# A first phase cut into other segments, sums in contiguous columns, and unread products on TensorE

## The chip, the cores and the metric

The kernel runs on one core of a Trainium2 chip. The metric is the time of one execution on the device, in microseconds (us). Three runs of the kernel before gave 1920.49, 1921.16 and 1923.17, so the median is 1921.16.

## What is computed

One layer of a hybrid decoder, for 256 prompt tokens and 8 samples of 8 tokens, 320 tokens in all (NT). The model width is 2048: 16 tiles (T) of 128 channels.

```python
mod = silu(c) @ ada_w + ada_b               # six sections of 2048: shift, scale, gate, twice
h   = rmsnorm(x, norm_mix_w) * (1 + sc_m) + sh_m
p   = h @ w_in                              # GLU value | GLU gate | z | x,B,C (3072 columns) | dt
xbc, new_sconv = causal_dwconv(xbc, st_sconv, ssm_conv_w, ssm_conv_b)   # 4 taps
y   = gated_rmsnorm(ssd_scan(silu(xbc), dt, ...), z)
v   = silu(layernorm(causal_dwconv(glu(value, gate))))                   # 31 taps
x   = x + g_m * (concat[v, y] @ w_out)
x   = x + g_f * conv_ffn(rmsnorm(x) * (1 + sc_f) + sh_f)
return rmsnorm(x), ...                      # and the last rows of each convolution, the SSD states
```

The outputs that carry the convolution states (`new_sconv` among them) hold the last three raw rows of x/B/C.

## The kernel before

**Products.** All data is fp32. Each weight tile is split into a high part (`whi`, ScalarE casts at L298 and L299, one for each half of its columns) and a low part (`wlo`, VectorE subtractions at L303 and L304), each h tile into `HQh` and `HQl`. A tile of 128 by 128 weights takes three matmuls of 320 columns: high by high (L378), high by low (L379), low by high (L380).

**The stream.** All weight loads stand in one list, `stream`. SyncE issues them in this order as soon as a buffer of the `raw` pool is free, and TensorE takes its work in the same order. There are two kinds of entry. A *unit* (kind "w") is a weight load of up to 2048 columns with its split and its matmuls. A *piece* (kind "ada") is a load of ada_w columns and unsplit matmuls of it with silu(c) into the bank `adaq` (L439).

**The first phase.** The scale and shift of an h tile must be known before h can be formed, so the kernel works by segments of h tiles, listed in `SEGS` as (first tile, number): 1, 3, 4, 4 and 4 tiles. For each segment there are pieces for its shift and scale (`KPIECE` k-slices in each, so 16/KPIECE pieces), then a chain that forms its h tiles, then units that multiply these tiles with their rows of the x/B/C weights. There are 24 output tiles; a unit holds `NUNIT` of them as *groups*, each group a sum over the segment's tiles in one of four `acc` banks of PSUM. The string of a segment in `orders` gives the stream: W is one of this segment's units, A one of the next segment's pieces. In the segments of 3 and 4 tiles the last A is followed by two W.

**The chain.** When the last piece is done, `chain` goes ahead of the other background work: a transpose and three small operations on VectorE (L446 to L452), then `modulated` (L230 to L244), which multiplies x by scale and by rstd, adds shift, lets ScalarE write `HQh` and VectorE write `HQl`. `bg.drain` places the steps of the background between the split of the next unit and the evictions: a unit first evicts what the unit before left, splits the next unit's weights, drains, and then issues its matmuls. `finish` in `pre` of the next segment's first unit makes sure that its h is formed.

**Evictions.** `xbc_evac` adds a group's bank into `extZ` (output tiles 0 to 13) or `extV` (14 to 23, named `rv` in the trace). There a tile has 347 columns: 3 of left padding, 256 of the prompt, and 8 samples with 3 state columns and 8 tokens each. So an eviction is two instructions, one of 256 columns (L516, L519) and one of 64 (L517, L520), copies on ScalarE in the first segment, additions on VectorE in the others. Groups but the last four of a unit are evicted two groups later (`each`), the last four at the start of the next unit. `pads` fills the state columns with two large GpSimd copies at the start of the last segment. In the last segment each second eviction adds the 4-tap convolution of two output tiles to the background (`xbc_conv`). The dt projection (`dt_product`, L580) runs ahead of the last segment's first unit.

Of the kernel before, what the change touches and what calls it, by code (L numbers as in the profile page):

```python
# [41 lines left out]
V0, C0 = VOFF["nfw"][0], COFF["idn"][0]  # L42


SEGS = [(0, 1), (1, 3), (4, 4), (8, 4), (12, 4)]

KPIECE = {1: 8, 3: 2, 4: 2}
NUNIT = {1: 6, 3: 4, 4: 4}
LAST = len(SEGS) - 1

POOLED = (2, 6)

# [53 lines left out]
def kernel(ctx: ExitStack, tc: tile.TileContext, A: dict):  # L106
# [48 lines left out]
    class Stats:  # L155
# [20 lines left out]
        def rstd(self, eps, collect=True):  # L176
# [3 lines left out]
            V.reciprocal(r, r)  # L180
            return r

    class Sums:


# [101 lines left out]
            slots.append(e["slot"])  # L287
        pump()

    def split(e, bgq=0.0):  # L290
        if "hi" in e:
            return
        w = e["w"]
        e["hi"] = sb.tile([128, w], F32R, tag="whi", name="whi", bufs=2)
        e["lo"] = sb.tile([128, w], F32R, tag="wlo", name="wlo", bufs=2)
        hw = (w // 256) * 128
        r0, r1 = e["raw"](0, hw), e["raw"](hw, w - hw)
        S.copy(e["hi"][:, :hw], r0)  # L298
        S.copy(e["hi"][:, hw:], r1)  # L299
        E = e.get("lo_on", V)  # L300
        if bgq and E is V:
            bg.drain(bgq)
        E.tensor_tensor(e["lo"][:, :hw], r0, e["hi"][:, :hw].bitcast(F32), op=ALU.subtract)  # L303
        E.tensor_tensor(e["lo"][:, hw:], r1, e["hi"][:, hw:].bitcast(F32), op=ALU.subtract)  # L304
        if bgq and E is G:
            bg.drain(bgq)
        release_raw(e)
# [22 lines left out]
    def run_stream():  # L330
# [7 lines left out]
        for n, e in enumerate(stream):  # L338
# [21 lines left out]
                bg.drain(0.65 * b)  # L360
            else:
                bg.drain(b)
            if "hi" not in e:
                split(e)
            xo = e["x"]() if callable(e["x"]) else e["x"]
            hi, lo = e["hi"], e["lo"]
            banks = []
# [18 lines left out]
                    pend.append(lambda f=e["each"], i=i, b=banks[i]: f(i, b))  # L386
            if e.get("evac"):
                pend.append(lambda f=e["evac"], bk=banks: f(bk))
            if m is not None and "hi" not in stream[m] and "raw" in stream[m]:
                split(stream[m])  # L390
            if e.get("post"):
                e["post"]()
# [31 lines left out]
    def ada_segment_entries(si):  # L424
# [18 lines left out]
        def chain():  # L443
            ps = get()
            md = scr("md")
            V.transpose(md[:, :w], ps[:, :w])  # L446
            m4 = md[:, :w].rearrange("p (s t r) -> p s t r", s=2, t=n)
            sc, sh = mods["s1"][:, t0:t0 + n, :], mods["sh1"][:, t0:t0 + n, :]
            bc = [128, n, 9]
            V.tensor_tensor(sc, m4[:, 0, :, 0:9], cv("adb", 16 + t0, n).unsqueeze(2).to_broadcast(bc), op=ALU.add)  # L450
            V.tensor_tensor(sh, m4[:, 1, :, 0:9], cv("adb", t0, n).unsqueeze(2).to_broadcast(bc), op=ALU.add)
            V.scalar_tensor_tensor(sc, sc, 1.0, cv("nmw", t0, n).unsqueeze(2).to_broadcast(bc),  # L452
                                   op0=ALU.add, op1=ALU.mult)
            yield 1.0
            if t0 % 4 == 0:
                box["parts"] = new_quarter(t0 // 4)
            box.setdefault("h", [None] * T)
            yield from modulated(t0, n, box["rstd_x"], mods["s1"], mods["sh1"], box["htmp"], box["h"], box["parts"])

        def post():  # L460
            bg.items.insert(0, [f"hq{si}", chain(), 0])
            if si == 0:
                bg.finish("hq0")

        np_ = T // kp
        for pc in range(np_):
# [42 lines left out]
    def xbc_evac(tb, q):  # L509
        def go(i, bank):  # L510
            tt = tb + i
            ext = xt_ext(tt)
            p, s, st = ext_views(ext, 3, 11)
            bs = v3(bank[:, NPR:NT], LS)
            if q == 0:
                S.copy(p, bank[:, :NPR])  # L516
                S.copy(s, bs)  # L517
            else:
                V.tensor_tensor(p, p, bank[:, :NPR], op=ALU.add)  # L519
                V.tensor_tensor(s, s, bs, op=ALU.add)  # L520
            if q == LAST and i % 2 == 1:
                bg.add("xconv" if tt >= 14 else "xconvz", xbc_conv(tt - 1))
                if tt == 13:
                    SP.dma_start(A["osc"][:, 0:14, :], box["extZ"][:, :, 256:347])
                if tt == 23:
                    SP.dma_start(A["osc"][:, 14:24, :], box["extV"][:, :, 256:347])
# [583 lines left out]
    with tc.manual_schedule():  # L1110
# [29 lines left out]

        aq = [ada_segment_entries(i) for i in range(len(SEGS))]

        st = Stats()
        for q, tag in enumerate(("HQh2", "HQl2", "HQh3", "HQl3")):
            sq = sb.tile([128, 4, NT], F32, tag=tag, name="sq" + tag)
# [17 lines left out]
        stream.extend(aq0)  # L1163
        hget = lambda: box["h"]
        NX = 24
        orders = ["WAAWAAWAAAWA", "WAAAAWWAAWAAWW", "AWAAWAAWAAWAWW", "AWAAWAAWAAWAWW", "WWWWWW"]
        W1 = A["w1"]
        for si, (t0, n) in enumerate(SEGS):
            nxt = list(aq[si + 1]) if si + 1 < len(SEGS) else []
# [2 lines left out]
            for ch in orders[si]:  # L1172
# [7 lines left out]
                def pre(si=si, g=g, t0=t0, n=n):  # L1180
                    if g == 0:
                        bg.finish(f"hq{si}")
                        if t0 + n in (8, 12):
                            raw_retire(f"q{(t0 + n) // 4}")
                    if (si, g) == (LAST, 0):
                        raw_retire("bc")
                    if (si, g) == (LAST, 1):
                        raw_retire("xs")
                    if (si, g) == (LAST, 0):
                        pads()  # L1190
# [11 lines left out]
        def pads():  # L1202
            for ext, a, b in ((zx, 0, 14), (vx, 14, 24)):
                G.memset(ext[:, :, 0:3], 0.0)
                pad = ext[:, :, 259:347].rearrange("p t (b s) -> p t b s", s=11)[:, :, :, 0:3]
                G.tensor_copy(pad, sst[:, 24 * a:24 * b].rearrange("p (t b s) -> p t b s", b=NB, s=3))

        stream[40]["also"] = late_loads

# [359 lines left out]
```

## Time and profile before

| | us |
|---|---|
| median of three runs | 1921.16 |
| the profiled execution, its own time | 1924.55 |
| its span from first to last instruction | 1922.8 |
| TensorE busy | 1866.0 |
| VectorE busy | 1160.1 |
| ScalarE busy | 866.1 |
| GpSimd busy | 478.7 |
| data moved | 395.85 MB |

TensorE is busy for 97% of the span. "Busy" counts a matmul at whatever clock was granted, so a window's row shows the granted clock (PEclk, a share of full speed) beside it. The first phase ends near 255 us of the span; the rest of the program is not touched by the change. A timeline row gives the start, the duration, the instruction, and in brackets the idle time of its engine just before it with what ended it.

### The profile page before, as it was taken

The numbers are of one execution on the slowest core, as the hardware profiler recorded it, in microseconds if no ns is written. First come the engines' busy times: TensorE is split into PE (matmuls) and PEld (weight loads), VectorE is DVE, ScalarE is ACT, GpSimd is POOL, SyncE is SP. The second block draws the span as 40 slices with busy tenths as digits, with TensorE's granted clock in tenths as the row PEclk, the third lists the DMA queues.
The fourth block names the chain that finished last, engine by engine and source line by source line (L and its number), as shares of the span: only waits on it lengthen the run. The fifth ranks groups of instructions, "written<-read, shape, count | busy, mean of one in ns | idle before, by whom it ended". The sixth has DMA issues, their size and how long they took to land.

```text
span 1922.8 us, 32409 instructions
## 1 busy us (share of the span) xinstructions
PE 1866.0 (97%) x13152; PEld 1748.0 (91%) x13152; DVE 1160.1 (60%) x2051; ACT 866.1 (45%) x1405; POOL 478.7 (25%) x558
## 2 busy tenths in 40 slices
PE   6999999999999999999999999999999999999997
PEld 4889888888888788899988999999999999999996
DVE  2665686786887478865475555544555544555544
ACT  5222475655554463343354444334445323444442
POOL 0000426667777764603100000000000000000010
PEclk9999999999999999999999999999999999999998
DMA  9986449777777767774367434444343443434441
GB/s 376 391 310 246 107 156 340 271 270 255 262 250 266 251 237 263 257 261 173 132 249 262 177 137 144 153 164 154 133 157 141 154 162 136 163 141 154 154 151 75
DMA packets 81206, 395.85 MB, mean 206 GB/s; under 512 B 13056, under 2 KB 28704, under 8 KB 44448
## 3 DMA queue, kind: packets, MB, share of 16 engines
q1 hardware_dynamic: 78704, 391.11, 56.8%
q10 hardware_dynamic: 2352, 2.66, 0.4%
q8 instruction: 104, 1.70, 0.4%
q14 instruction: 46, 0.38, 0.1%
HBM read 374.35 MB, written 19.39 MB: 205 GB/s over the span
## 4 chain that ended last, share of the span: by engine, by line
PE 86%; DVE 4%; DMA 3%; POOL 3%; ACT 2%; issue 1%; SPq 0%; ACTq 0%; DVEq 0%; POOLq 0%
PE acc L378 27%; PE acc L380 26%; PE acc L379 26%; PE ada L478 3%; PE adaq L439 1%; DMA rx<-in_wxs_dram 1%; DVE wlo L304 1%; DMA raw<-in_ads_dram 1%; DVE wlo L303 1%; DMA zraw<-in_w_dram 1%; PE yps L818 1%; DMA rb<-in_ads_dram 0%; ACT whi L298 0%; POOL Vt L744 0%; DMA X<-in_xT_dram 0%
## 5 line engine op out<-in xcount | busy, mean ns | idle before, releaser
L378 PE MATMUL acc<-HQh,whi 128*128 128x320 f32 x3072 | 964.3, 314 | 13.7 <-ACT whi L298 3.9
L379 PE MATMUL acc<-HQl,whi 128*128 128x320 f32 x3072 | 953.4, 310 | 2.1 <-DVE HQl L1266 1.8
L380 PE MATMUL acc<-HQh,wlo 128*128 128x320 f32 x3072 | 953.6, 310 | 1.3 <-DVE wlo L303 0.7
L378 PEld LDWEIGHTS acc<-HQh,whi 128*128 128x128 f32 x3072 | 580.8, 189 | 57.1 <-issue 22.2
L379 PEld LDWEIGHTS acc<-HQl,whi 128*128 128x128 f32 x3072 | 580.9, 189 | 3.2 <-DVE HQl L1266 2.0
L380 PEld LDWEIGHTS acc<-HQh,wlo 128*128 128x128 f32 x3072 | 580.4, 189 | 2.1 <-POOL wlo L303 1.1
L298 ACT CAST whi<-raw 128x1024 fp32r<-128x1024 f32 (+2 forms) x164 | 168.8, 1029 | 229.2 <-PE acc L379 174.0
L303 DVE TENSOR_TENSOR wlo<-raw,whi 128x1024 fp32r<-128x1024 f32 (+2 forms) x141 | 171.3, 1215 | 98.8 <-ACT whi L298 93.6
L1095 DVE SCALAR_TENSOR_TENSOR ft<-ft,cvec 128x336 f32<-128x336 f32 x176 | 88.3, 564 | 215.6 <-ACT ft L1089 215.6
L380 PE MATMUL acc<-ah,wlo 128*128 128x320 f32 x704 | 217.5, 309 | 0.0
L378 PE MATMUL acc<-ah,whi 128*128 128x320 f32 x704 | 217.5, 309 | 0.0
L379 PE MATMUL acc<-al,whi 128*128 128x320 f32 x704 | 217.5, 309 | 0.0
L1090 POOL COPY nfs<-ft 128x2 f32<-128x2 f32 x88 | 18.4, 209 | 777.0 <-ACT ft L1077 777.0
L304 DVE TENSOR_TENSOR wlo<-raw,whi 128x1024 fp32r<-128x1024 f32 (+2 forms) x141 | 173.5, 1230 | 0.0
L299 ACT CAST whi<-raw 128x1024 fp32r<-128x1024 f32 (+2 forms) x164 | 168.6, 1028 | 0.0
L378 PEld LDWEIGHTS acc<-ah,whi 128*128 128x128 f32 x704 | 132.2, 188 | 0.0
L379 PEld LDWEIGHTS acc<-al,whi 128*128 128x128 f32 x704 | 132.2, 188 | 0.0
L380 PEld LDWEIGHTS acc<-ah,wlo 128*128 128x128 f32 x704 | 132.2, 188 | 0.0
L706 DVE SCALAR_TENSOR_TENSOR cva<-rt,cvec,cva 128x320 f32<-128x320 f32 x240 | 131.8, 549 | 0.0
L706 DVE SCALAR_TENSOR_TENSOR cvb<-rt,cvec,cvb 128x320 f32<-128x320 f32 x208 | 114.3, 549 | 0.0
L1039 DVE SCALAR_TENSOR_TENSOR X<-acc,mod_g,X 128x256 f32<-128x256 f32 x64 | 31.0, 484 | 135.7 <-PE acc L380 135.6
L1077 ACT COPY ft<-acc 128x256 f32<-128x256 f32 x88 | 32.7, 371 | 171.7 <-PE acc L380 170.5
(305 smaller groups left out, 1886.7 us busy)
## 6 DMA issues: line engine op xcount, KB each, us to landing
raw<-in_wu_dram SPq DMA_DIRECT2D x63, 1024.0 KB, 4.8
raw<-in_ada_dram SPq DMA_DIRECT2D x43, 1024.0 KB, 5.9
raw<-in_w_dram SPq DMA_DIRECT2D x26, 1024.0 KB, 5.1
zraw<-in_w_dram SPq DMA_DIRECT2D x21, 1024.0 KB, 5.0
rt<-in_wu_dram SPq DMA_DIRECT2D x21, 1024.0 KB, 4.8
raw<-in_wd_dram SPq DMA_DIRECT2D x24, 896.0 KB, 4.5
raw<-in_wo_dram SPq DMA_DIRECT2D x16, 1024.0 KB, 7.1
zraw<-in_ada_dram SPq DMA_DIRECT2D x14, 1024.0 KB, 6.9
```

Of the source, the lines that this page charges most:

```text
L298: S.copy(e["hi"][:, :hw], r0)
L299: S.copy(e["hi"][:, hw:], r1)
L303: E.tensor_tensor(e["lo"][:, :hw], r0, e["hi"][:, :hw].bitcast(F32), op=ALU.subtract)
L304: E.tensor_tensor(e["lo"][:, hw:], r1, e["hi"][:, hw:].bitcast(F32), op=ALU.subtract)
L378: PE.matmul(ps[:, :NT], hi[:, s:s + 128], xh, start=st, stop=False)
L379: PE.matmul(ps[:, :NT], hi[:, s:s + 128], xl, start=False, stop=False)
L380: PE.matmul(ps[:, :NT], lo[:, s:s + 128], xh, start=False, stop=sp)
L478: PE.matmul(ps[32 * j:32 * j + 32, :], csil[:, k, :], raw(512 * j, 512), start=(k == 0), stop=(k == 15))
L706: V.scalar_tensor_tensor(v3(v, LS) if k == 29 else d, tap(k), w(k), d, op0=ALU.mult, op1=ALU.add)
L1039: V.scalar_tensor_tensor(X[0][:, t, :NPR], bank[:, :NPR], mods[g][:, t, 0:1], X[0][:, t, :NPR], op0=ALU.mult, op1=ALU.add)
L1077: S.copy(pr, bank[:, :NPR])
L1095: V.scalar_tensor_tensor(acc, ext[:, k:k + 336], cv("fdw", 3 * n + k), acc, op0=ALU.mult, op1=ALU.add)
```

## The change

- The segments are 1, 2, 4, 5 and 4 tiles, with 8, 4, 2, 1 and 2 k-slices in a piece and 6, 6, 4, 3 and 4 output tiles in a unit. A segment that reaches over a quarter of h (tiles 3 to 6, 7 to 11) calls `modulated` twice, once for each quarter.
- `orders` is new: behind the last piece now stands one unit, not two.
- `busy(n)` issues n fp32 matmuls (128 by 128, 256 columns) into a bank that nobody reads: six ahead of the statistics of x, five behind the first segment's chain.
- `split_hi` casts the first unit's high part ahead of the first segment's chain.
- While they are summed, the 320 columns of a tile lie contiguously at columns 27 to 346 (`run`). An eviction is one copy, on ScalarE and VectorE in turn (first segment), or one addition on VectorE (the middle ones). In the last segment the two additions move the sum into the padded places, and GpSimd copies the three state columns of each sample, one copy for each tile, in place of the two large ones of `pads`.
- Buffers are lent and given back at other entries (`raw_retire`), and the constants of the later phases are loaded at entry 42 in place of 40.

```diff
-SEGS = [(0, 1), (1, 3), (4, 4), (8, 4), (12, 4)]
-KPIECE = {1: 8, 3: 2, 4: 2}
-NUNIT = {1: 6, 3: 4, 4: 4}
+SEGS = [(0, 1), (1, 2), (3, 4), (7, 5), (12, 4)]
+KPIECE = {1: 8, 2: 4, 4: 2, 5: 1}
+NUNIT = {1: 6, 2: 6, 4: 4, 5: 3}
...
+    def busy(n):
+        ps = ax_bank("busy")
+        for _ in range(n):
+            PE.matmul(ps[:, :256], cs("one"), csil[:, 0:8, :].rearrange("p a b -> p (a b)"), start=True, stop=True)
...
-            if t0 % 4 == 0:
-                box["parts"] = new_quarter(t0 // 4)
-            yield from modulated(t0, n, box["rstd_x"], mods["s1"], mods["sh1"], box["htmp"], box["h"], box["parts"])
+            a = t0
+            while a < t0 + n:
+                b = min(t0 + n, a // 4 * 4 + 4)
+                if a % 4 == 0:
+                    box["parts"] = new_quarter(a // 4)
+                yield from modulated(a, b - a, box["rstd_x"], mods["s1"], mods["sh1"], box["htmp"], box["h"], box["parts"])
+                a = b
...
             if si == 0:
+                split_hi(next(e for e in stream if e["kind"] == "w"))
                 bg.finish("hq0")
+                busy(5)
...
-            bs = v3(bank[:, NPR:NT], LS)
+            run = ext[:, 27:347]
             if q == 0:
-                S.copy(p, bank[:, :NPR])
-                S.copy(s, bs)
+                (S.copy if i % 2 == 0 else V.tensor_copy)(run, bank[:, :NT])
+            elif q < LAST:
+                V.tensor_tensor(run, run, bank[:, :NT], op=ALU.add)
             else:
-                V.tensor_tensor(p, p, bank[:, :NPR], op=ALU.add)
-                V.tensor_tensor(s, s, bs, op=ALU.add)
+                V.tensor_tensor(p, run[:, :NPR], bank[:, :NPR], op=ALU.add)
+                V.tensor_tensor(s, v3(run[:, NPR:NT], LS), v3(bank[:, NPR:NT], LS), op=ALU.add)
+                G.tensor_copy(st, v3(sst[:, 24 * tt:24 * tt + 24], 3))
...
+        busy(6)
         st = Stats()
...
-        orders = ["WAAWAAWAAAWA", "WAAAAWWAAWAAWW", "AWAAWAAWAAWAWW", "AWAAWAAWAAWAWW", "WWWWWW"]
+        orders = ["WAWAWAAW", "AWAAWAAWAAAW", "AAWAAAWAAAWAAAWAAAWAAW", "AWAWAWAWAWAWAWAW", "WWWWWW"]
...
-                        if t0 + n in (8, 12):
-                            raw_retire(f"q{(t0 + n) // 4}")
-                    if (si, g) == (LAST, 0):
+                        if si in (2, 3):
+                            raw_retire(f"q{si}")
+                    if (si, g) == (LAST - 1, 3):
                         raw_retire("bc")
-                    if (si, g) == (LAST, 1):
+                    if (si, g) == (LAST - 1, 6):
                         raw_retire("xs")
...
-                pad = ext[:, :, 259:347].rearrange("p t (b s) -> p t b s", s=11)[:, :, :, 0:3]
-                G.tensor_copy(pad, sst[:, 24 * a:24 * b].rearrange("p (t b s) -> p t b s", b=NB, s=3))
-        stream[40]["also"] = late_loads
+        stream[LATE]["also"] = late_loads
```

Where VectorE passes to the third segment, the kernel before has the transpose of the modulation (L446), the low part of the segment's first unit, the four tiles' modulation up to the sum that ScalarE rounds (L236), and then the evictions of the last segment's last but one unit:

```order
L446 STREAM_TRANSPOSE md<-adaq 128x256
L450 TENSOR_TENSOR mod_s_65<-md,cvec 128x36
L451 TENSOR_TENSOR mod_sh_66<-md,cvec 128x36
L452 SCALAR_TENSOR_TENSOR mod_s_65<-mod_s_65,cvec 128x36
L303 TENSOR_TENSOR wlo<-rh_130,whi 128x768
L304 TENSOR_TENSOR wlo<-rl_131,whi 128x768
L230 TENSOR_TENSOR rt_82<-X,mod_s_65 128x4x64
L231 TENSOR_TENSOR rt_82<-rt_82,rstd 128x4x64
L233 TENSOR_TENSOR rt_82<-rt_82,mod_sh_66 128x4x64
L236 SCALAR_TENSOR_TENSOR rt_82<-X,mod_s_65,rstd 128x256 x4
L519 TENSOR_TENSOR rv_84<-rv_84,acc 128x256
```

VectorE at the same place of the changed kernel, from the low part of the third segment's first unit on:

```order
L318 TENSOR_TENSOR wlo<-rh_137,whi 128x1024
L319 TENSOR_TENSOR wlo<-rl_138,whi 128x1024
L238 TENSOR_TENSOR rt_82<-X,mod_s_65 128x64
L239 TENSOR_TENSOR rt_82<-rt_82,rstd 128x64
L241 TENSOR_TENSOR rt_82<-rt_82,mod_sh_66 128x64
L244 SCALAR_TENSOR_TENSOR rt_82<-X,mod_s_65,rstd 128x256
L249 TENSOR_TENSOR HQl_238<-rt_82,HQh_237 128x64
L252 SCALAR_TENSOR_TENSOR HQl_238<-rt_82,mod_sh_66,HQh_237 128x256
L238 TENSOR_TENSOR rt_82<-X,mod_s_65 128x3x64
...
L249 TENSOR_TENSOR HQl_766<-rt_82,HQh_765 128x3x64
L252 SCALAR_TENSOR_TENSOR HQl_766<-rt_82,mod_sh_66,HQh_765 128x256 x2
L538 TENSOR_TENSOR rv_84<-rv_84,acc 128x320 x6
```

The modulation is in two calls, one tile and three, and the evictions (L538, here those of the unit behind the last piece) stand behind both, with a 1024-column split in place of 768 ahead of them.

On VectorE at the passage to the fourth segment the changed kernel has, behind the 320-column transpose:

```order
L318 TENSOR_TENSOR wlo<-raw_1094,whi 128x960
L319 TENSOR_TENSOR wlo<-raw_1094,whi 128x960
L238 TENSOR_TENSOR rt_82<-X,mod_s_65 128x64
...
L252 SCALAR_TENSOR_TENSOR HQl_766<-rt_82,mod_sh_66,HQh_765 128x256
L238 TENSOR_TENSOR rt_82<-X,mod_s_65 128x4x64
L239 TENSOR_TENSOR rt_82<-rt_82,rstd 128x4x64
L241 TENSOR_TENSOR rt_82<-rt_82,mod_sh_66 128x4x64
L244 SCALAR_TENSOR_TENSOR rt_82<-X,mod_s_65,rstd 128x256 x4
L538 TENSOR_TENSOR rv_84<-rv_84,acc 128x320 x4
L249 TENSOR_TENSOR HQl_1267<-rt_82,HQh_1266 128x4x64
```

One whole tile of h (six rows from L238 to L252) has come in ahead of the four-tile modulation, and so ahead of the four evictions.

On GpSimd in the last segment the kernel before has two large copies into the state columns (L1206) ahead of the dt chain, and behind the chain the taps of the pooled convolutions (L547) in one row. The changed kernel has:

```order
L570 TENSOR_TENSOR xacc<-xacc 128x344 x2
L543 COPY extZ<-rt_82 128x8x3 x8
L570 TENSOR_TENSOR xacc<-xacc 128x344 x4
L543 COPY extZ<-rt_82 128x8x3 x2
L543 COPY rv_84<-rt_82 128x8x3 x2
L570 TENSOR_TENSOR xacc<-xacc 128x344 x2
L543 COPY rv_84<-rt_82 128x8x3 x4
```

The copies (L543) now stand between the taps (L570), each behind the additions of its own tile on VectorE.

## Rows read from the trace of the kernel before

**Rows 1.** The page: busy time of each engine; a group: busy, mean ns

```profile
PE 1866.0 (97%) x13152; PEld 1748.0 (91%) x13152; DVE 1160.1 (60%) x2051; ACT 866.1 (45%) x1405; POOL 478.7 (25%) x558
L1090 POOL COPY nfs<-ft 128x2 f32<-128x2 f32 x88 | 18.4, 209 | 777.0 <-ACT ft L1077 777.0
```

**Rows 2.** Windows: us; busy of PE, PEld, DVE, ACT, POOL; PEclk; DMA share; GB/s

```profile
20.00:66.80 46.80, 38.29 (x374) 32.51 (x363) 20.90 (x55) 22.15 (x70) 0.00 (x0) 0.89 1.03 407
66.80:80.00 13.20, 13.20 (x129) 10.96 (x127) 7.43 (x20) 3.36 (x5) 0.00 (x0) 1.00 1.02 413
36.00:37.00 1.00, 0.00 (x0) 0.00 (x0) 0.00 (x0) 0.48 (x2) 0.00 (x0) 1.00 1.01 385
50.00:51.00 1.00, 1.00 (x5) 1.00 (x5) 0.00 (x0) 0.00 (x0) 0.00 (x0) 0.50 1.02 418
```

**Rows 3.** Timeline, ScalarE, waiting for the weights of a unit: start, us, instruction, idle

```profile
52.99 0.83 ACT L298 CAST whi<-raw 128x768 fp32r<-128x768 f32 x1 [4.39 <-DMA raw<-in_wxs_dram]
```

**Rows 4.** Timeline, TensorE, first phase

```profile
23.29 0.64 PE L378 MATMUL acc<-HQh,whi 128*128 128x320 f32 x1 [2.90 <-ACT whi L298]
...
37.94 0.41 PE L378 MATMUL acc<-HQh,whi 128*128 128x320 f32 x1 [2.21 <-ACT extZ L517]
...
47.85 0.63 PE L378 MATMUL acc<-HQh,whi 128*128 128x320 f32 x1 [3.06 <-ACT HQh L238]
...
65.84 0.31 PE L378 MATMUL acc<-HQh,whi 128*128 128x320 f32 x1
...
70.53 0.31 PE L380 MATMUL acc<-HQh,wlo 128*128 128x320 f32 x1
...
78.11 1.07 PE L439 MATMUL adaq<-raw,csil 128*32 128x256 f32 x16
79.00 0.61 PE L439 MATMUL adaq<-rh,csil 128*32 128x256 f32 x8
...
86.21 0.39 PE L378 MATMUL acc<-HQh,whi 128*128 128x320 f32 x1 [0.69 <-ACT HQh L238]
...
179.00 0.42 PE L378 MATMUL acc<-HQh,whi 128*128 128x320 f32 x1
...
193.27 0.74 PE L580 MATMUL dtp<-HQh,rx 128*32 128x320 f32 x8
...
196.52 0.72 PE L580 MATMUL dtp<-HQh,rx 128*32 128x320 f32 x8
```

**Rows 5.** Timeline, VectorE: modulation of one tile, of three, and passages before

```profile
21.16 0.22 DVE L230 TENSOR_TENSOR rt<-X,mod_s 128x64 f32<-128x64 f32 x1
...
23.27 0.56 DVE L303 TENSOR_TENSOR wlo<-raw,whi 128x384 fp32r<-128x384 f32 x1
...
45.72 0.36 DVE L230 TENSOR_TENSOR rt<-X,mod_s 128x192 f32<-128x192 f32 x1
...
48.23 1.27 DVE L244 SCALAR_TENSOR_TENSOR HQl<-rt,mod_sh,HQh 128x256 fp32r<-128x256 f32 x3
...
85.52 0.42 DVE L519 TENSOR_TENSOR rv<-rv,acc 128x256 f32<-128x256 f32 x1
...
179.96 1.22 DVE L303 TENSOR_TENSOR wlo<-raw,whi 128x1024 fp32r<-128x1024 f32 x1
...
182.23 0.42 DVE L230 TENSOR_TENSOR rt<-X,mod_s 128x256 f32<-128x256 f32 x1
...
185.07 0.42 DVE L519 TENSOR_TENSOR rv<-rv,acc 128x256 f32<-128x256 f32 x1
...
187.26 1.67 DVE L244 SCALAR_TENSOR_TENSOR HQl<-rt,mod_sh,HQh 128x256 fp32r<-128x256 f32 x4
```

**Rows 6.** Timeline, last segment: a TensorE wait, a GpSimd copy, a VectorE subtraction

```profile
241.05 0.38 PE L378 MATMUL acc<-HQh,whi 128*128 128x320 f32 x1 [1.24 <-DVE rv L520]
...
194.00 1.36 POOL L1206 COPY rv<-rt 128x240 f32<-128x240 f32 x1 [1.77 <-DVE rv L520]
...
194.98 1.42 DVE L304 TENSOR_TENSOR wlo<-rx,whi 128x1024 fp32r<-128x1024 f32 x1
```

More of the change, by code (lines that the diff above doesn't have):

```diff
@@ L42 @@
 V0, C0 = VOFF["nfw"][0], COFF["idn"][0]
-SEGS = [(0, 1), (1, 3), (4, 4), (8, 4), (12, 4)]
-KPIECE = {1: 8, 3: 2, 4: 2}
-NUNIT = {1: 6, 3: 4, 4: 4}
+SEGS = [(0, 1), (1, 2), (3, 4), (7, 5), (12, 4)]
+KPIECE = {1: 8, 2: 4, 4: 2, 5: 1}
+NUNIT = {1: 6, 2: 6, 4: 4, 5: 3}
 LAST = len(SEGS) - 1
+LATE = 42
 POOLED = (2, 6)
@@ L288, in release_raw, with split_hi @@
         pump()
-    def split(e, bgq=0.0):
-        if "hi" in e:
-            return
+    def split_hi(e):
         w = e["w"]
@@ L295, in split @@
         e["lo"] = sb.tile([128, w], F32R, tag="wlo", name="wlo", bufs=2)
-        hw = (w // 256) * 128
+        hw = w // 2
+        S.copy(e["hi"][:, :hw], e["raw"](0, hw))
+        S.copy(e["hi"][:, hw:], e["raw"](hw, w - hw))
+    def split(e, bgq=0.0):
+        if "lo_done" in e or e.get("product"):
+            return
+        w = e["w"]
+        hw = w // 2
         r0, r1 = e["raw"](0, hw), e["raw"](hw, w - hw)
-        S.copy(e["hi"][:, :hw], r0)
-        S.copy(e["hi"][:, hw:], r1)
+        if "hi" not in e:
+            split_hi(e)
+        e["lo_done"] = True
         E = e.get("lo_on", V)
@@ L362, in run_stream @@
                 bg.drain(b)
-            if "hi" not in e:
-                split(e)
+            split(e)
             xo = e["x"]() if callable(e["x"]) else e["x"]
@@ L388, in run_stream @@
                 pend.append(lambda f=e["evac"], bk=banks: f(bk))
-            if m is not None and "hi" not in stream[m] and "raw" in stream[m]:
+            if m is not None and "raw" in stream[m]:
                 split(stream[m])
```

## The prediction

> **What bounds the kernel now.** I read the page first: TensorE is busy 97% of the span [rows 1]. So the time can only change where TensorE idles or runs at a lower granted clock, and, since the change ends with the first phase, a microsecond that the start of the later work moves by is a microsecond of the span. Next the windows [rows 2]. From 20 to 66.8 us TensorE is busy 38.29 of 46.80 at a granted clock of 0.89, while the DMA engines are busy without a break (share 1.03, 407 GB/s): this stretch waits for weights. From 66.8 to 80 it is busy 13.20 of 13.20 at full clock. The timelines say where the idle time is: 2.90 us before the first unit, 2.21 at 37.94, 3.06 at 47.85, and a last 0.69 at 86.21 [rows 4]. The wait for weights itself is plainest on ScalarE, which stands 4.39 us until a DMA lands at 52.99 [rows 3]. After 3.06 us of idle TensorE runs at 0.50 of its clock (50 to 51); after the 2.21 us it does not (36 to 37, clock 1.00, and no half clock behind it) [rows 2]. Last, VectorE at the passages between segments [rows 5], since there its order decides when a bank comes free.
>
> A matmul of 320 columns takes 0.147 us in a row (65.84 to 70.53, 32 of them [rows 4]). A piece of ada_w takes 0.89 (78.11 to 79.00).
>
> **The start: the segments and the DMA.** The first segments become smaller (1 and 2 tiles in place of 1 and 3), so TensorE gets work from fewer weights. The loads still come in stream order at the same rate. In the order of the change, VectorE evicts the third unit of the second segment behind the low part of the fourth. Counting columns in the stream, 33792 must land for that, against 26624 for the landing at 52.99; 7168 columns of 128 rows and 4 bytes are 3.67 MB, at 407 GB/s 9.0 us: 62.0. Add one cast (0.86, from the 0.83 of [rows 3]) and the two subtractions of 768 columns (1.75, three quarters of the 2.27 from 179.96 to 182.23 [rows 5]): 64.6. An eviction is about 0.5 (0.42 for 256 columns [rows 5]); then the unit's last two groups follow, 12 matmuls, 1.8: the unit ends at 66.9. Work done by then: first segment 72 matmuls, 10.6; three quarters of 144 for the second, 15.9; its four pieces, 4.2 (an estimate: twice the matmuls of half the width, over 0.89); five pieces of the third segment, 4.4: 35.1. The kernel before has done by 80.0, when its last piece ends: 10.6, two thirds of 216 matmuls (21.2), 8 pieces of four tiles (6.9) and 8 of three (5.6, an estimate by the same way), 44.3; less the 13.2 since 66.8 that is 31.1. So the change is **3.9 us ahead** at that point. One transfer of 1 MB more or less is 2.6 us, of which about half reaches TensorE: 2.5 to 5.5.
>
> That includes all that happens earlier. The earlier cast of the first unit, the single copies for two, and the unread products (which may save some of the half clock behind 23.29) make TensorE wait longer for the same weights, and add nothing here.
>
> **The passage from 2 to 4 tiles.** Call T the end of a segment's last piece. Behind it the kernel before has two units of four groups. Its passage to the last segment shows the times: T = 179.00 [rows 4]; 0.96 for the modulation's small operations, 2.27 for the split, 2.84 for the four tiles up to their sum, and at T + 6.07 the first eviction starts [rows 5]; TensorE has 48 matmuls, 7.05, in its four banks, and never waits. In the passage to the third segment the groups are of three tiles, 36 matmuls, 5.3, and TensorE waits the 0.69 of 86.21 with the eviction at 85.52 [rows 4, 5]. The change has one unit behind the last piece, of six groups of **two** tiles: four banks hold 24 matmuls, **3.5 us**. VectorE has ahead of the first eviction: 0.96, 2.27, a whole single tile 2.11 (21.16 to 23.27), then three tiles 2.51 (45.72 to 48.23) and two of their low parts, 0.84 (a third of 1.27 each) [rows 5]: 8.7, and 0.5 for the eviction, 9.2. So TensorE stands for **5.6 us** (4.5 to 6.5: the single tile's 2.11 holds waits for ScalarE that may overlap). An idle time longer than the 3.06 should bring the half clock; the mean clock of 0.89 over 46.8 us is 5.1 us of lost clock for the two idle times at 23.29 and 47.85, of which I give the second up to 3.2; the 2.21 us cost nothing [rows 2]. I take **2.0** (0 to 3.2). The 0.69 of before is gone: -0.7.
>
> **The passage from 4 to 5 tiles.** One unit of 7.05 and one piece of 0.89: TensorE is covered to T + 7.9. VectorE: 0.96, 2.13 for 960 columns, 2.11 for tile 7, 2.84, and 0.5: the first bank is free at T + 8.5. The low part of tile 8 is queued behind four evictions, T + 10.9, and TensorE meets it after three matmuls. Idle 0.6 and 1.9, **2.4** taken (1.0 to 3.5). Here the trace of before has no idle time.
>
> **The passage from 5 to 4 tiles.** The last unit is three groups of 15 matmuls, 6.6. Then the dt product: three quarters of it take 3.25 (193.27 to 196.52 [rows 4]), so the last quarter comes at T + 9.9 and its low parts at T + 10.4. VectorE has two of the four sums behind the evictions, which wait for T + 6.6, and the low parts of the last two tiles behind a split of 2.27: about T + 12. Idle **1.5** (0.5 to 2.5). Before, all four low parts (187.26, 1.67 long [rows 5]) were done well ahead of 193.27.
>
> **The last segment.** TensorE waits there for an eviction (1.24 at 241.05 [rows 6]), so VectorE bounds part of it. The second addition of a tile now waits for the first, about 0.1 for each of 24 tiles. GpSimd gets 24 copies between the taps; the nearest small one takes 0.21 [rows 1], so 5 us of its time in place of the large copies (1.36 [rows 6]), and the eight ahead of the second pair's taps delay these by at most 1.7. A good part is hidden: **+1.0** (-0.5, if the copies that no longer stand ahead of the dt chain let it begin earlier, to 3). In the middle segments the single addition saves VectorE some 0.1 to 0.2 for each eviction, hidden since TensorE is full there.
>
> The subtraction beside the large copy takes 1.42, without one 1.22 [rows 5, 6]. The Trainium skill, page SBUF — State Buffer, section Who interferes with whom, says that a VectorE instruction with two inputs in SBUF contends with a GpSimd instruction that reads SBUF, and the trace agrees by those 0.2 us. By it each copy could hold VectorE once, at most 24 times 0.2, 5 us in place of my 1.0.
>
> **The sum.** -3.9 + 5.6 + 2.0 - 0.7 + 2.4 + 1.5 + 1.0 = **+7.9 us**. Against the profiled execution, 1924.55, that is 1932.4. This execution is 3.4 above the median of the runs shown; on the median, 1921.16, the change gives **1929**. With all terms at their low ends (-5.5, 4.5, 0, -0.7, 1.0, 0.5, -0.5) the sum is -0.7, with all high (-2.5, 6.5, 3.2, -0.7, 3.5, 2.5, 3.0) +15.5. The likeliest case's own range is 1922 to 1936.
>
> **Rivals.**
> *The passages are covered* (faster). If VectorE reaches the first eviction within the four banks' 3.5 us, or the drain's order lets TensorE take other work, the lead of 3.9 is kept, the 0.7 too, and with the last segment at nothing the time is 1916.5, or 1914 with the larger lead and the last segment's low end. For it: in the passage of before at 179.00 TensorE stays full. Against: in the order of the change six evictions stand behind the whole chain, and 8.7 cannot become 3.5 by shorter waits. It decides if the chain's part ahead of the evictions is under about 5 us.
> *Half the waits* (no change). The steps overlap better than the rows let me add: idle 3.0 and 1.0 without a fall of the clock, the last passage hidden: -3.9 + 3.0 - 0.7 + 1.0 + 1.0, about +0.4: 1921.5.
> *The clock and the tail* (more slower). The half clock also follows the second passage (3), and GpSimd's copies delay VectorE's evictions and the taps by 4 in place of 1: 1929 + 6, 1935.
> *The unread products do not hold the clock.* Then the start runs at half clock as before, and, since the DMA sets the 66.9, nothing changes in the sum.
>
> **How the numbers follow.** My forecast 0.46, the clock and the tail 0.12, half the waits 0.18, passages covered 0.24. Two in ten may be left out: from the covered case's 1914 to 1937. A measurement of this kernel can tell some 0.2%, 3.8 us, from no change: faster 0.24, same 0.18, slower 0.58.
>
> **What would show it.** The third segment's first unit should stand behind an idle TensorE of 4.5 to 6.5 us near 73 us, ended by a VectorE eviction (L538), with a granted clock of 0.5 behind it; at the start of the fourth segment some 2 us, ended by an eviction and then by the low part of a tile. The second segment's third unit should end near 67 us with the DMA share still at 1. The forecast is wrong if the evictions come within 5 us of the last piece, if the lead at 67 us is 8 or more in place of 3.9, or if TensorE has little to do with VectorE there at all. Behind 260 us all windows should be as before, moved by a constant.

## The result, and the profile after

The changed kernel takes 1938.28 us (median of four runs, 1937.35 to 1940.33), 1.0085 times the kernel before (95% interval 1.0073 to 1.0098). Four runs of the kernel before, beside it, have a median of 1921.41, so it is 16.9 us slower. Forecast were 1929 and a range of 1914 to 1937. The sign was right, the size was half of what came, and the time lies just above the range.

The profiled execution took 1940.33 with a span of 1937.8, 15.0 longer than before. The page, and the windows that answer to the first two of [rows 2]:

```profile
PE 1873.7 (97%) x13174; PEld 1752.4 (90%) x13174; DVE 1167.0 (60%) x1999; ACT 862.0 (44%) x1371; POOL 486.4 (25%) x580
```

```profile
20.00:66.80 46.80, 40.82 (x389) 34.18 (x388) 28.87 (x61) 15.61 (x31) 0.00 (x0) 0.93 1.02 407
66.80:80.00 13.20, 7.80 (x80) 6.07 (x80) 9.77 (x26) 4.41 (x8) 0.00 (x0) 0.97 0.82 304
```

The page tells little: TensorE is busy 97% as before. The windows tell the first half of the story. Up to 66.8 us TensorE does more than before (40.82 us at a clock of 0.93, against 38.29 at 0.89), with the DMA as busy as before (share 1.02 against 1.03, 407 GB/s in both). From 66.8 to 80, where it was full, it now stands 5.4 of 13.2 us.

To see the second half, the same point of the program is looked up in both traces. The ScalarE timeline has such points: the copy of the first z unit's result, and the first sigmoid behind the GLU gate unit (Vt). Before:

```profile
259.30 0.43 ACT L753 COPY z<-acc 128x320 f32<-128x320 f32 x1 [4.02 <-PE acc L380]
...
294.56 0.44 ACT L670 ACTIVATE Vt<-acc 128x320 f32<-128x320 f32 x1
```

After:

```profile
268.36 0.43 ACT L776 COPY z<-acc 128x320 f32<-128x320 f32 x1 [4.25 <-PE acc L394]
...
307.47 0.44 ACT L693 ACTIVATE Vt<-acc 128x320 f32<-128x320 f32 x1
```

The first point has moved by 9.1 us, the second by 12.9. Behind the second the matmuls run at half clock for a while:

```profile
308.00:311.00 3.00, 3.00 (x13) 3.00 (x13) 0.00 (x0) 0.00 (x0) 1.81 (x1) 0.50 1.01 414
```

Twelve of them start 0.267 us apart in place of 0.147, which is 1.4 us more. The products behind the first phase are the same in both kernels, so their matmuls can be matched one by one, from the last one backwards. The distance between the two traces is 9.06 us for all matmuls of the z units, 13.86 behind the first GLU units, and 14.2 at the last matmul. So the first phase costs 9.1, near to the forecast (a second trace of the changed kernel, run e10 below, has 7.8 there), and **4.8 microseconds more are lost in the first GLU units, between 294 and 312 us, where the diff has not a line of arithmetic**.

The waits of TensorE in the changed kernel, from its timeline (start, duration, instruction, in brackets the idle time and what ended it):

```profile
43.93 0.41 PE L392 MATMUL acc<-HQh,whi 128*128 128x320 f32 x1 [3.16 <-ACT rv L536]
...
70.46 0.42 PE L392 MATMUL acc<-HQh,whi 128*128 128x320 f32 x1
...
79.65 0.64 PE L392 MATMUL acc<-HQh,whi 128*128 128x320 f32 x1 [5.40 <-DVE rv L538]
...
84.14 0.41 PE L392 MATMUL acc<-HQh,whi 128*128 128x320 f32 x1
...
137.34 0.39 PE L392 MATMUL acc<-HQh,whi 128*128 128x320 f32 x1 [0.49 <-ACT HQh L246]
139.17 0.42 PE L393 MATMUL acc<-HQl,whi 128*128 128x320 f32 x1 [1.01 <-DVE HQl L252]
...
205.17 1.12 PE L603 MATMUL dtp<-HQl,raw 128*32 128x320 f32 x4 [0.73 <-DVE HQl L252]
...
229.68 0.38 PE L392 MATMUL acc<-HQh,whi 128*128 128x320 f32 x1 [1.03 <-ACT whi L303]
...
249.88 0.38 PE L392 MATMUL acc<-HQh,whi 128*128 128x320 f32 x1 [0.86 <-DVE rv L542]
...
259.51 0.39 PE L392 MATMUL acc<-HQh,whi 128*128 128x320 f32 x1 [2.37 <-DVE rv L542]
...
296.57 0.42 PE L394 MATMUL acc<-HQh,wlo 128*128 128x320 f32 x1 [1.36 <-POOL wlo L318]
...
305.10 0.41 PE L392 MATMUL acc<-HQh,whi 128*128 128x320 f32 x1 [0.52 <-ACT whi L303]
...
307.54 0.42 PE L394 MATMUL acc<-HQh,wlo 128*128 128x320 f32 x1 [1.87 <-POOL wlo L318]
```

70.46 is the end of the last piece before the passage to the third segment, 84.14 the third segment's first matmul. The last three rows are where the loss comes that was not forecast: the GLU units wait for the low parts of their weights, which GpSimd makes, and once for ScalarE's high part. In the kernel before this stretch has two waits of 0.28 us.

VectorE between the last piece and the evictions, the place of the forecast's largest term:

```profile
71.43 1.22 DVE L318 TENSOR_TENSOR wlo<-rh,whi 128x1024 fp32r<-128x1024 f32 x1
...
73.70 0.22 DVE L238 TENSOR_TENSOR rt<-X,mod_s 128x64 f32<-128x64 f32 x1
...
75.81 0.35 DVE L238 TENSOR_TENSOR rt<-X,mod_s 128x192 f32<-128x192 f32 x1
...
79.11 1.68 DVE L538 TENSOR_TENSOR rv<-rv,acc 128x320 f32<-128x320 f32 x4
```

0.97 for the small operations, 2.27 for the split, 2.11 for the single tile, 3.30 for the three: 8.65, where the prediction had 8.7.

**Where the GLU units' weights are late.** The trail goes from GpSimd back to ScalarE (high part), to the DMA, and to SyncE, which can issue a load only when a buffer is free. Here are, after, the cast of the third z unit's weights, the split of the second z unit on VectorE with the wait behind it, and the loads on SyncE's queue. The row at 266.72 is the load of the third z unit:

```profile
272.84 1.05 ACT L303 CAST whi<-raw 128x1024 fp32r<-128x1024 f32 x1 [4.05 <-DMA raw<-in_w_dram]
```

```profile
265.48 1.21 DVE L319 TENSOR_TENSOR wlo<-raw,whi 128x1024 fp32r<-128x1024 f32 x1
...
273.92 1.22 DVE L318 TENSOR_TENSOR wlo<-raw,whi 128x1024 fp32r<-128x1024 f32 x1 [4.30 <-ACT whi L303]
```

```profile
247.22 0.34 SPq L289 DMA_DIRECT2D raw<-in_w_dram  x1
255.51 0.33 SPq L289 DMA_DIRECT2D raw<-in_ada_dram  x1
...
266.72 0.33 SPq L289 DMA_DIRECT2D raw<-in_w_dram  x1
```

And SyncE's queue in the kernel before, where the row at 238.52 is the load of the third z unit:

```profile
195.09 1.66 SPq L281 DMA_DIRECT2D rx<-in_w_dram  x2
196.85 1.32 SPq L281 DMA_DIRECT2D rx<-in_ada_dram  x2
...
238.52 0.34 SPq L281 DMA_DIRECT2D raw<-in_w_dram  x1
```

Before, the first z unit's weights and the piece behind it lie in `rx`, the buffers called xs (195.09 and 196.85), so the three raw buffers are one unit further ahead, and the third z unit's load is issued at 238.52. After, xs and bc are given back (`raw_retire`) three and five units earlier, nothing of the z stretch lies in them, and that load is issued at 266.72, the moment when VectorE has split the second z unit. VectorE then waits for it (4.30), its taps of the last convolutions come later, the next loads too, and the low part of the first GLU unit on GpSimd is started behind late weights and beside those taps.

### The profile page after: what moved, and what is told of

It reads as the page before. It is cut to its first block, busy times and chain, and to the rows that moved or that the text cites. A ratio compares the mean times of both kernels' runs of the same rounds, so it can differ in the third digit from the quotient of the medians.

```text
span 1937.8 us, 32334 instructions
## 1 busy us (share of the span) xinstructions
PE 1873.7 (97%) x13174; PEld 1752.4 (90%) x13174; DVE 1167.0 (60%) x1999; ACT 862.0 (44%) x1371; POOL 486.4 (25%) x580
## 4 chain that ended last, share of the span: by engine, by line
PE 59%; DVE 2%; DMA 1%; issue 0%; ACT 0%; SPq 0%; DVEq 0%; ACTq 0%; POOL 0%; POOLq 0%
PE acc L392 19%; PE acc L393 19%; PE acc L394 19%; PE ada L498 1%; DVE wlo L319 0%; DVE wlo L318 0%; DMA X<-in_xT_dram 0%; PE stp L963 0%; DMA raw<-in_ada_dram 0%; DVE X L1441 0%; DVE ssdv L965 0%; PE yot L989 0%; PE yop L1019 0%; DVE stb L958 0%; PE sum L212 0%
```

## The experiments

Ratios are to the kernel before, run beside each on the same chip, with their 95% intervals. The changed kernel itself was run a second time (run e10), with no edit:

> The changed kernel itself, beside the others on the same chip, as their reference: 1.0075 to 1.0098 times the kernel before; waits as in its trace (5.4 at the third segment, 4 us of ScalarE for the third z unit's weights).

1.0085 (1.0061 to 1.0108), the same ratio again.

**Is it the number of units behind the last piece?** (run e2)

```diff
-orders = ["WAWAWAAW", "AWAAWAAWAAAW", "AAWAAAWAAAWAAAWAAAWAAW", "AWAWAWAWAWAWAWAW", "WWWWWW"]
+orders = ["WAWAWAAW", "AWAAWAAAAAWW", "AAWAAAWAAAWAAAAAWAAAWW", "AWAWAWAWAWAWAAWW", "WWWWWW"]
```

> The changed kernel with other orders only: in the second, third and fourth segment two units stand behind the last piece, as in the kernel before; the number of units and pieces is the same. Theory A: the waits of the passages (5.40 us, 1.5 of half clock, 1.5, 0.73) are due to there being one unit, so that the four banks are full before VectorE has formed the next h. Then the 5.40 is gone, the waits together are under 1 us, and the time is 1928 to 1931. Theory B: VectorE's longer chain (two calls of the modulation) is what costs, whatever stands behind the last piece: then the idle time moves into the second unit and 4 us or more of it stay: 1934 or more.

1.0108 (1.0093 to 1.0123), 1940.51 us: no faster than the changed kernel, if anything slower (the intervals just touch). TensorE's waits there:

```profile
62.55 0.64 PE L392 MATMUL acc<-HQh,whi 128*128 128x320 f32 x1 [4.67 <-DVE extZ L538]
...
80.37 0.63 PE L392 MATMUL acc<-HQh,whi 128*128 128x320 f32 x1 [4.88 <-DVE extZ L538]
```

The wait of the passage stays (4.88), now inside the first of the two units, and pieces that are crowded ahead of them bring a new one (4.67). Since the edit also moves pieces, its time alone would not decide; the place of the 4.88 does. Theory A falls. A second unit is no cover when the first can't leave its banks: what hides VectorE's chain is the work that fits in four banks, as in the prediction's 3.5 us.

**Is it the banks?** (run e5)

```diff
-groups=[(acc_bank, list(range(t0, t0 + n)), True, True) for _ in range(nt)],
+groups=[(ax_bank if si == 1 and i >= 4 else acc_bank, list(range(t0, t0 + n)), True, True) for i in range(nt)],
```

> The changed kernel with one edit: in the segment of two tiles the fifth and sixth group of a unit are summed in two banks of the other PSUM pool (ax), so that such a unit has six banks, not four. Theory A: TensorE stands 5.40 us at 79.65 because its four banks hold only 3.5 us of work in groups of two tiles. With six, the unit behind the last piece runs through (5.3 us) and two pieces follow (1.2), so that the idle time falls to 2.0 to 3.5 us, the half clock behind it (12 matmuls, 1.5 us) goes or shrinks, and the third segment's first matmul comes 3 to 4.5 us earlier than at 84.14: 1933.5 to 1936. Theory B: what is missing is the h of the third segment itself, so that its first matmul stays near 84: 1937 to 1939.

1.0062 (1.0045 to 1.0078). TensorE at the passage, the third segment's first two waits:

```profile
79.51 0.38 PE L392 MATMUL acc<-HQh,whi 128*128 128x320 f32 x1 [2.53 <-ACT whi L303]
81.80 0.41 PE L393 MATMUL acc<-HQl,whi 128*128 128x320 f32 x1 [0.59 <-DVE HQl L252]
```

The third segment begins at 79.51, not 84.14, 4.6 us earlier (3 to 4.5 were expected); the idle time is 3.1 in place of 5.4, and the granted clock is 1.00 from 79 to 84. The interval just touches that of the changed kernel, but the trace shows the gain in its place: theory A stands.

**Is the late loss a matter of buffers?** First one edit that was too small (run e1):

```diff
-                    if (si, g) == (LAST - 1, 6):
+                    if (si, g) == (LAST, 0):
                         raw_retire("xs")
```

> The changed kernel with one edit: the xs buffers are taken out of the pool of load buffers at the last segment's first unit, not three units before it (with both pools given back as late as before, the kernel can't run; this is one load further ahead in the last segment). Theory A: the 5 us that come in between 268 and 308 us come from weight loads that are issued too late because the pool is small too early. Then the wait of ScalarE for weights at 272.84 (4.05 us) and TensorE's waits at 296.57, 305.10 and 307.54 (1.36, 0.52, 1.87) shrink, and the time is 1933 to 1935 against 1938.3 of the changed kernel. Theory B: they come from GpSimd, whose low parts of the first GLU units are slow (5.84 us at 290.68) or stand behind its copies. Then the loads move and TensorE's waits stay: 1937 to 1939.

1.0086 (1.0069 to 1.0103): nothing gained. By the trace the edit missed its aim. The loads of the last segment's own units moved into rx, but the third z unit's load was still issued at 265.49, and ScalarE still waited for it:

```profile
271.17 1.05 ACT L303 CAST whi<-raw 128x1024 fp32r<-128x1024 f32 x1 [5.18 <-DMA raw<-in_w_dram]
```

So this run did not tell the theories apart. The next one (run e6) gives xs back one unit later still, `(LAST, 1)`, where the kernel before has it:

```diff
-                    if (si, g) == (LAST - 1, 6):
+                    if (si, g) == (LAST, 1):
                         raw_retire("xs")
```

> The changed kernel with the xs buffers given back at the last segment's second unit, as in the kernel before, in place of the segment ahead of it; by this the second ada load of the z stretch lies in rx, and the loads of the z units come in the order and buffers of the kernel before. Theory A (the loads are issued too late since the pool is small too early): the weights of the third z unit are issued some 20 us earlier than at 266.72, ScalarE no longer waits 4.05 us for them, and TensorE's 1.36, 0.52 and 1.87 us around 296 to 308 fall under 1 us in all: 1933 to 1935. Theory B (GpSimd's slow low parts, independent of the loads): 1937 to 1939.

1.0058 (1.0035 to 1.0081). The third z unit's load on SyncE's queue:

```profile
254.15 0.34 SPq L289 DMA_DIRECT2D raw<-in_w_dram  x1
```

That is 12.6 us earlier, not 20: it stands behind the store of the convolution state (242.64), and goes out when a buffer comes free. ScalarE has no wait for it. TensorE is full from 260 to 300, and one wait is left:

```profile
260.00:300.00 40.00, 40.00 (x277) 34.84 (x276) 28.52 (x48) 26.18 (x60) 11.06 (x7) 1.00 0.65 207
```

```profile
302.21 0.41 PE L394 MATMUL acc<-HQh,wlo 128*128 128x320 f32 x1 [1.68 <-POOL wlo L318]
```

Under 1 us of waits was expected, so 1.68 is more than that. And the other way round, the kernel before with the early return alone (run e7):

```diff
-                    if (si, g) == (LAST, 0):
+                    if (si, g) == (LAST - 1, 2):
                         raw_retire("bc")
-                    if (si, g) == (LAST, 1):
+                    if (si, g) == (LAST - 1, 4):
                         raw_retire("xs")
```

> The kernel before with one edit: the bc and xs buffers are given back at the third and fifth unit of the fourth segment, not at the first two units of the last, so that the loads of the z stretch stand in the changed kernel's buffers. Theory A: the weights come late there as in the changed kernel, and the first GLU units wait: 1924.5 to 1927. Theory B: the buffers are of no account: 1920 to 1922.5.

1.0026 (1.0014 to 1.0039), some 5 us slower than the kernel before, with segments, sums and everything else untouched. The same waits appear, on ScalarE and then on TensorE:

```profile
262.09 1.05 ACT L298 CAST whi<-raw 128x1024 fp32r<-128x1024 f32 x1 [5.10 <-DMA raw<-in_w_dram]
```

```profile
285.97 0.41 PE L380 MATMUL acc<-HQh,wlo 128*128 128x320 f32 x1 [2.56 <-POOL wlo L303]
...
296.58 0.42 PE L380 MATMUL acc<-HQh,wlo 128*128 128x320 f32 x1 [1.88 <-POOL wlo L303]
```

The intervals of e6 and of the changed kernel overlap a little, so the traces are asked too, by the matched matmuls of the section on the result. From the z units to behind the first GLU units, the changed kernel loses 4.8 us against the kernel before in both of its traces. e1 to e5 and e7, which all give xs back before the last segment's second unit, lose 4.0 to 4.4. The four that give it back there lose at most 0.9: e6 0.85, and e8, e9 and e11, which stand below, nothing. e6 and e9 still give bc back early, so it is xs that counts. The buffers are shown from both sides.

**Do the unread products do anything?** Both uses of `busy` are left out (run e3):

```diff
-                busy(5)
...
-        busy(6)
```

> The changed kernel without the unread products of busy(6) and busy(5). Theory A: the first 67 us are paced by the DMA, so that TensorE's clock there is of no account: 1938 plus or minus 1.5, and the first unit behind the wait at 43.93 begins within 0.5 us of where it did. Theory B: the unread products keep the clock up and TensorE's early units set the pace: 1940 to 1943.

1.0082 (1.0067 to 1.0097), as the changed kernel. They do make TensorE faster at first. The same eight matmuls of the statistics, without them and then with them:

```profile
11.18 1.29 PE L163 MATMUL stat<-sqHQl,cst 128*32 128x320 f32 x8 [0.31 <-ACT sqHQl L1168]
```

```profile
10.18 0.75 PE L163 MATMUL stat<-sqHQl,cst 128*32 128x320 f32 x8 [0.85 <-ACT sqHQl L1170]
```

The granted clock reads 1.00 around both rows, so the durations alone tell it. The first unit begins at 23.19 without them and at 21.27 with them. Yet the unit behind the long wait begins at 42.67 without them and at 43.93 with them, 1.3 apart where theory A allowed 0.5: what was won is waited off again, in a stretch where ScalarE's casts wait for weights in both (1.15 us before 36.87 without them, 1.94 before 37.32 with them).

**The contiguous sums.** In the changed kernel, the old evictions and the two large GpSimd copies (run e4):

```diff
-            run = ext[:, 27:347]
+            bs = v3(bank[:, NPR:NT], LS)
             if q == 0:
-                (S.copy if i % 2 == 0 else V.tensor_copy)(run, bank[:, :NT])
-            elif q < LAST:
-                V.tensor_tensor(run, run, bank[:, :NT], op=ALU.add)
+                S.copy(p, bank[:, :NPR])
+                S.copy(s, bs)
             else:
...
+                V.tensor_tensor(p, p, bank[:, :NPR], op=ALU.add)
+                V.tensor_tensor(s, s, bs, op=ALU.add)
...
+                G.tensor_copy(pad, sst[:, 24 * a:24 * b].rearrange("p (t b s) -> p t b s", b=NB, s=3))
```

> The changed kernel with the sums of the kernel before: two instructions for each eviction, into the padded places, copies on ScalarE alone in the first segment, and the two large GpSimd copies into the state columns. Theory A: the contiguous sums cost about 1 us in the last segment and save 0.1 for an eviction in the passages: 1936.5 to 1939. Theory B: the 24 GpSimd copies, which the store of the convolution state on the SyncE queue waits for, hold up the weight loads behind it: then the loads behind the first store go out earlier and the time is 1932 to 1935.

1.0099 (1.0080 to 1.0117), no gain. And in the kernel before, the new sums alone (run e11):

```diff
-            bs = v3(bank[:, NPR:NT], LS)
+            run = ext[:, 27:347]
...
+            elif q < LAST:
+                V.tensor_tensor(run, run, bank[:, :NT], op=ALU.add)
...
+                G.tensor_copy(st, v3(sst[:, 24 * tt:24 * tt + 24], 3))
...
```

> The kernel before with the contiguous sums alone (single copies and additions in the first four segments, GpSimd's 24 copies in the last), its own segments and buffers and no unread products. Theory A: the sums are worth less than 1 us: 0.9995 to 1.0008 times the kernel before. Theory B: they make up the 1.9 us of the run with old segments: 1.0008 to 1.002.

0.9997 (0.9986 to 1.0008). The sums are worth nothing that can be told from zero.

**All but the segments.** The changed kernel with the old segments, orders and buffers, and the late constants again at entry 40 (run e8):

```diff
-SEGS = [(0, 1), (1, 2), (3, 4), (7, 5), (12, 4)]
+SEGS = [(0, 1), (1, 3), (4, 4), (8, 4), (12, 4)]
...
-        orders = ["WAWAWAAW", "AWAAWAAWAAAW", "AAWAAAWAAAWAAAWAAAWAAW", "AWAWAWAWAWAWAWAW", "WWWWWW"]
+        orders = ["WAAWAAWAAAWA", "WAAAAWWAAWAAWW", "AWAAWAAWAAWAWW", "AWAAWAAWAAWAWW", "WWWWWW"]
...
-                    if (si, g) == (LAST - 1, 3):
+                    if (si, g) == (LAST, 0):
                         raw_retire("bc")
-                    if (si, g) == (LAST - 1, 6):
+                    if (si, g) == (LAST, 1):
                         raw_retire("xs")
```

> The changed kernel with the segments, pieces, units, orders and places of the returned buffers of the kernel before; the contiguous sums, the unread products and the earlier cast stay. Theory A: the cost of the change lies in the segments (passages and pieces) and in the returned buffers, the rest is worth less than 1.5 us either way: 1919.5 to 1923. Theory B: the contiguous sums and GpSimd's copies cost several us in the last segment: 1924 or more.

1.0010 (1.0001 to 1.0020), 1.9 us, at the edge of being told from nothing. So about 1.0085 - 1.0010, some 14 us, are the segments and the returned buffers. What the 1.9 is made of stays open; the sums alone did not show it.

**The two causes together**, banks and buffers mended, no unread products (run e9):

```diff
-                busy(5)
...
-        busy(6)
...
-                    if (si, g) == (LAST - 1, 6):
+                    if (si, g) == (LAST, 1):
                         raw_retire("xs")
...
-groups=[(acc_bank, list(range(t0, t0 + n)), True, True) for _ in range(nt)],
+groups=[(ax_bank if si == 1 and i >= 4 else acc_bank, list(range(t0, t0 + n)), True, True) for i in range(nt)],
```

> The changed kernel with the six banks of the two-tile units, the xs buffers given back as late as in the kernel before, and without the unread products. Theory A (the two costs are separate and add up): the ratio to the kernel before falls from 1.0085 by the 0.0023 of the banks and the 0.0027 of the buffers to 1.003 to 1.004, some 1928 us; what is left are the waits of the two later passages, the dearer pieces of five tiles and the last segment. Theory B (one wait hides behind the other, so that a lead won early is lost again at the late weights): 1.0055 or more, as each edit alone.

1.0045 (1.0028 to 1.0061). Each edit alone gave 0.0023 and 0.0027, together 0.0040: they add up but for 0.001, which the intervals allow. Beside e10, on the same chip, the gain is plain: its four runs take 1930.72 to 1933.42 us, those of the changed kernel 1936.03 to 1942.16. No wait of the passage to the third segment beyond 3.1 us is left, and of the GLU waits this:

```profile
298.75 0.41 PE L394 MATMUL acc<-HQh,wlo 128*128 128x320 f32 x1 [0.29 <-POOL wlo L318]
```

It is the best version of the changed kernel, and still slower than the kernel before.

## Why the prediction went wrong, by its own steps

| step | forecast, us | measured, us |
|---|---|---|
| lead at the end of the DMA-paced start | -3.9 | -4.2 |
| passage 2 to 4 tiles, idle | 5.6 | 5.40 |
| half clock behind it | 2.0 | 1.3 |
| the 0.69 of before | -0.7 | gone |
| passage 4 to 5 tiles | 2.4 | 1.50 |
| passage 5 to 4 tiles | 1.5 | 0.73 |
| last segment | 1.0 | 0.5 |
| more work in pieces | none | 2.3 |
| behind 260 us | none | 4.8 |

**The start** came as worked out. The cast of the fourth unit's weights began at 60.70, behind 6.07 us of waiting for the DMA (62.0 forecast), the third unit ended at 67.6 (66.9). The lead, by the same count at 70.46 with all pieces at their measured times: 180 matmuls, 26.5; two pieces of one tile, 2.8; four of two, 5.2; eight of four, 8.3; 42.8 in all. The kernel before has 48.1 at 80.0 (31.8, 3.2, 5.8 and 7.3), and so was at 74.7 where the changed one was at 70.46.

**The large passage** came within 0.2 us, since every duration was in the trace of before. The granted clock was 0.50 behind it, as forecast:

```profile
80.00:82.00 2.00, 2.00 (x9) 2.00 (x9) 1.14 (x3) 0.00 (x0) 0.00 (x0) 0.50 0.00 0
```

It cost ten matmuls (80.08 to 82.48) some 0.12 us each, 1.3 with the steps at both ends. One reading of the prediction holds only for its place: that 2.21 us of idle time cost nothing. Its window, 36 to 37, lies inside the idle time (the clock is 1.00 from 38 to 44 too), but behind the 2.14 us at 250.46 the kernel before has 0.50 from 252 to 255, and behind the 2.51 at 34.20 the changed kernel has 0.50 from 35 to 38. The length of the idle time alone does not tell whether the clock falls. In the sum this changes nothing, since the first 67 us are paced by the DMA and the last segment has such a wait in both kernels. In the two smaller passages, where no half clock came, VectorE's times held within 0.3 us (the first eviction was forecast to be done 8.5 us behind the last piece, and was at about 8.7; the last tiles' low parts at about 12, and were at 11.9), but TensorE came to the place 0.5 to 0.9 us later than I had counted, and so waited less. The 0.49 at 137.34 was ended by ScalarE's `HQh`, where the forecast had an eviction. In the last segment the waits are 1.03 + 0.86 + 2.37, against 0.41, 1.24 and 2.14 before.

**The pieces** are a term that I left out. The prediction starts from "the time can only change where TensorE idles or runs at a lower granted clock"; but TensorE's own work changed too. Without their waits all pieces of the first phase take TensorE 33.8 us in the changed kernel and 31.6 in the kernel before; behind the lead's point it is 17.5 against 15.2. Sixteen of 320 columns take 9.4 us, and eight of 256, one segment's worth before, 7.6. I had priced a five-tile piece where it covered something, and never summed it as work.

These terms give 6.8; the shift at the first z unit is 9.1. About 0.8 of the rest is the dt product's last part, whose four matmuls behind the 0.73 take 1.05 us (205.17 to 206.22), where eight take 0.54 in [rows 4] (six such rows in 3.25). About as much again comes from changing between units and pieces: behind the lead's point the changed kernel has 14 stretches of pieces, the kernel before 10, and each costs some 0.19 (67.50 to 67.73 and 70.46 to 70.71, in place of 0.147 each). 0.7 stays unexplained by single rows. That the first phase came near to the forecast is therefore in part luck: the forecast's own terms measure 4.5 in place of 7.9, and what it left out adds about as much again.

**The step that failed** is the sentence "Behind 260 us all windows should be as before, moved by a constant". It treated the edits of `raw_retire` as bookkeeping, with no price, and so did the remark ahead of it that the change does not touch the program behind 255 us. They take four buffers (three of xs, one of bc) from the load pool three and five units earlier; that is paid one stretch later, when three buffers carry z units and pieces in turn, and a load can go out only when VectorE has split the unit before. The order of SyncE's queue showed it in advance: of the loads of the z stretch two stand in rx before, none after. I looked at the queue for the loads of the first 67 us, and not behind the last segment. e6 and e7 give the price as 5 us by their ratios, and as 4.0 and 4.1 by their traces.

The range went wrong with it: its dearest rival, a worse clock and tail at 1935, came out milder, and no case in the range stood for a later stretch. Without the 4.8 us the time would have lain inside.

## What to carry to other kernels

When a change gives buffers back earlier, follow the issuing queue to the first load that no longer finds one, and price what waits for that load, even if it lies a hundred microseconds behind the edit. The cover for a chain on another engine is the work that fits in the banks that are free, not the number of units queued behind it; smaller groups shrink it, more banks restore it. A lead at a stretch that the DMA paces can be lost in the next passage: here 4.2 us were won, and 5.4 of idle time with 1.3 of half clock lost. And a change that cuts work into other pieces has its own work to be summed, not only the waits.

## What the hardware showed

GpSimd's subtraction stands nearly still beside VectorE's taps. The same subtraction of 128 by 1024 on GpSimd, in the changed kernel beside the taps and then alone, and the taps on VectorE:

```profile
290.68 5.84 POOL L318 TENSOR_TENSOR wlo<-raw,whi 128x1024 fp32r<-128x1024 f32 x1 [26.63 <-ACT whi L303]
296.47 2.40 POOL L319 TENSOR_TENSOR wlo<-raw,whi 128x1024 fp32r<-128x1024 f32 x1
```

```profile
284.46 9.84 DVE L576 SCALAR_TENSOR_TENSOR xacc<-rv,cvec,xacc 128x344 f32<-128x344 f32 x20
```

The taps end at 294.30, 3.62 us behind the subtraction's start, and the subtraction takes 3.44 longer than its neighbour. The same two rows of the kernel before:

```profile
279.26 4.60 POOL L303 TENSOR_TENSOR wlo<-raw,whi 128x1024 fp32r<-128x1024 f32 x1 [25.14 <-ACT whi L298]
```

```profile
271.75 9.84 DVE L553 SCALAR_TENSOR_TENSOR xacc<-rv,cvec,xacc 128x344 f32<-128x344 f32 x20
```

There 2.3 us overlap; in e6 the subtraction takes 5.74 with 3.5. The extra time is nearly the overlap each time, while a tap takes 0.49 us beside it and alone. So late weights cost a little twice here: they push VectorE's taps further into GpSimd's work. By the two durations that is an estimated 1.2 of the 4.8 us. The Trainium skill, page SBUF — State Buffer, section Who interferes with whom, says that a VectorE instruction with two inputs in SBUF contends with a GpSimd instruction that reads SBUF; the trace agrees, and shows GpSimd as the one that waits. For the 24 small copies, where the prediction had weighed the same rule, e4 and e11 show no price.
